# A pair's middle result taken by ScalarE before the seventh product, and its sum of weights formed by GpSimd

## The chip, the cores and the metric

The kernel runs on one core of a Trainium2 chip. The metric is the device time of one execution, in microseconds (us); shorter is better. Five engines work side by side, each through its own queue in order, and wait for one another by semaphores: TensorE (PE in the profile, its weight loads PEld), VectorE (DVE), ScalarE (ACT), GpSimd (POOL) and SyncE (SP), which here issues DMAs.

## The reference

One layer of a hybrid decoder: 16 meta tokens stand before 512 tokens of width 1024, and on the same RMS-normalised stream run a differential softmax attention and a chunked gated DeltaNet, whose gated outputs are merged. Cut to what matters:

```python
hn = rms_norm(h, norm_w)                       # 528 x 1024
proj = hn @ w_in                               # 1024 x 10256, split into:
aq, ak, av, az, dq, dk, dv, dz, db, da, ga, gd
y_a = (rms_norm(diff_attention(aq, ak, av)) * silu(az)) @ w_branch_attn
y_d = (rms_norm(gated_delta(l2(conv(dq)), l2(conv(dk)), conv(dv), ...)) * silu(dz)) @ w_branch_delta
h = h + (sigmoid(ga) * y_a + sigmoid(gd) * y_d) @ w_out
out = rms_norm(h, final_norm_w)[:, 16:]
```

Everything is float32. The change touches how blocks of `hn @ w_in` (`ak`, `av`, and most of `dk`, `dv`, `dq`) and the two branch products are computed, not what is computed.

## The kernel before, in words

**Tiles and passes.** `w_in` comes in blocks of 128 output channels, each 1024x128, held as a 128x1024 tile `raw`. To keep float32 accuracy, weights and activations are each split in a high part (`wh`, `hnH`) and a low part (`wl`, `hnL`), and a product of one 128-row slice is three matmuls: high by high, low activations by high weights, high activations by low weights (`PASSES`). ScalarE makes `wh` by a copy (a CAST of 128x1024), VectorE makes `wl` by a subtraction.

**Pairs of blocks.** Two neighbouring blocks are computed together, with seven half-size products in place of eight (Strassen's scheme in Winograd's form). The 528 tokens are cut into halves of 264 (`HALF`), the 1024 input channels into two halves. 17 pairs of `w_in` go through `pair_of_blocks`, 8 pairs of the branch weights through `pair_products`. A product is 4 slices by 3 passes, 12 matmuls of 264 columns. They run in this order, each with its accumulator in PSUM, the weights it takes, their half, and the half or sum of activations:

```python
PRODUCTS = dict(p1=("r", "wa", 0, "b11"), p2=("s", "wa", 1, "b21"), p6=("r", "wb", 1, "t2"), p5=("t", "wb", 0, "t1"),
                p7=("r", "wc", 0, "t3"), p4=("r", "wc", 1, "t4"), p3=("t", "wd", 0, "b22"))
PAIR_PRODUCTS = {**PRODUCTS, "p4": ("q", "wc", 1, "t4")}
```

So p3 is the seventh product, and it adds to the accumulator "t" that p5, the fourth, has filled. Out of the accumulators come four quarters of result: block 0 takes a copy of r after p1 plus s, and a copy of r after p6 plus t after p3; block 1 takes a copy of r after p7 (the tile `cn`, copied by ScalarE in `snap_c`) plus q, and the same `cn` plus t as it stands **before** p3. The quarters go to a tile `xp` (for blocks that a convolution follows) or `vT` (attention keys and values). `total` is the VectorE addition that makes a quarter. For the last quarter named, `total(1, 1, "t", "c", cn)`, p3 has to wait: the dense work yields `c+` until that addition has read t, and the addition itself waits for `cn`, which waits for p7.

**The sums of weights.** `split_pair` holds both raw blocks, `a1` and `a2`, and forms in VectorE additions of 128x512 the weights wb (in the tile `st`), wc (over `a2`) and wd (over half of `a1`: `raw<-raw,st` in the profile). wd is formed only after the low part of wa was made, since wa is read from the same place. Then follow its cast on ScalarE (`wh<-raw` 128x512) and its low part on VectorE (`wl<-raw,wh` 128x512). Only p3 takes wd. There are three pairs of buffers W for split weights, and wd's comes free when p2 is done.

**What sets the order.** Tasks are written as generators. A planner (`Plan`) runs them against its own table of instruction costs and hops between engines and writes each engine's instructions down in the order in which they would start; a task that waits for an event or a buffer lets others go ahead. So a change of who waits for what moves instructions of all the other tasks (DeltaNet chunks, attention heads, gates) around it. `th` is a kind of buffer of two 128x512 tiles (slices of the tile `room`), which the gates' tanh uses; its two slots are first given out when the sums of activations t1 to t4 have been formed.

Of the kernel before, what the change touches and what calls it, by code (L numbers as in the profile page):

```python
# [14 lines left out]
ALU = mybir.AluOpType  # L15
# [18 lines left out]
def dense_order():  # L34

    order = []
    for g in range(H // 2):
        k, v, q, z = ([(n, 2 * g), (n, 2 * g + 1)] for n in ("dk", "dv", "dq", "dz"))
        a0, a1 = ([(n, 2 * g + i) for n in ("ak", "av", "aq", "az")] for i in range(2))
        order += k + v + (a0 + q + a1 + z if g else q + a0[2:3] + z[:1] + a0[:2] + a0[3:] + z[1:] + a1)  # L40
    order += [("gd", c) for c in range(KB)] + [("ga", 0)]
    for n in range(KB):
        order += [("ga", n + 1)] * (n < KB - 1) + [(("yd", "ya")[n // 4], 2 * (n % 4) + i) for i in range(2)]
    return order
# [6 lines left out]
                p7=("r", "wc", 0, "t3"), p4=("r", "wc", 1, "t4"), p3=("t", "wd", 0, "b22"))  # L51
# [6 lines left out]
ORDER = dense_order()  # L58
# [3 lines left out]
HALF = L // 2  # L62
# [6 lines left out]
PE, DVE, ACT, POOL, SP = "PE", "DVE", "ACT", "POOL", "SP"  # L69
# [19 lines left out]
class Plan:  # L89
# [176 lines left out]
def hybrid_block(ctx: ExitStack, tc: tile.TileContext, x, meta, wblk, wbd, wout, pcol, prow, out):  # L266
    nc = tc.nc
    plan = Plan({**SLOTS, "wo": 0, "th": 0}, BANKS, ALL_BANKS)
    T, V, A, G, S = (Engine(plan, n, e) for n, e in
                     ((PE, nc.tensor), (DVE, nc.vector), (ACT, nc.scalar), (POOL, nc.gpsimd), (SP, nc.sync)))  # L270
    spawn, done = plan.spawn, plan.done
# [127 lines left out]
    st = mk(wp, [P, D], F32, "st")  # L399
# [29 lines left out]
    def split_pair(n, two):  # L429

        (a1, i1), (a2, i2) = two
        h0, h1, both = slice(0, D // 2), slice(D // 2, D), slice(0, D)
        name = (ORDER[n][0], ORDER[n][1] // 2) if ORDER[n][0] in ("yd", "ya") else n
        pairs[name] = tiles = {}

        def sums():
            yield ("st",)
            yield DVE
            V.tensor_tensor(out=st[:, h0], in0=a2[:, h0], in1=a2[:, h1], op=ALU.add)
            yield DVE  # L440
            V.tensor_tensor(out=st[:, h1], in0=st[:, h0], in1=a1[:, h0], op=ALU.subtract)
            done(f"wb sum {name}")
            yield DVE
            V.tensor_tensor(out=a2[:, h0], in0=a1[:, h0], in1=a2[:, h0], op=ALU.subtract)
            done(f"wc sum {name}")
            yield f"wa {name}"
            yield DVE
            V.tensor_tensor(out=a1[:, h1], in0=a1[:, h1], in1=st[:, h1], op=ALU.subtract)
            done(f"wd sum {name}")
            if tick(f"st {name}", 2):  # L450
                give("st")

        def low(key, src, cols, which):
            wh, wl = Ws[which]
            yield DVE
            V.tensor_tensor(out=wl[:, cols], in0=src, in1=wh[:, cols].bitcast(F32), op=ALU.subtract)
            tiles[key] = wh, wl, which
            done(f"{key} {name}")
            if key == "wb":
                if tick(f"st {name}", 2):  # L460
                    give("st")
            elif key != "wa":
                plan.give("raw", i2 if key == "wc" else i1)

        if n:
            yield f"took {n - 1}"
        spawn(sums())
        for key, src, cols in (("wa", a1, both), ("wb", st, both), ("wc", a2, both), ("wd", a1[:, h1], h0)):
            if key != "wa":
                yield f"{key} sum {name}"  # L470
            yield ("W",)
            which = plan.task.slot
            yield ACT
            A.copy(out=Ws[which][0][:, cols], in_=src)
            spawn(low(key, src, cols, which))
        done(f"took {n + 1}")
# [380 lines left out]
    ths = [room[3][:, n, 0:SEQ] for n in range(SLOTS["th"])]  # L857
# [11 lines left out]
    cn = mk(dp, [P, HALF], F32, "cn")  # L869
# [811 lines left out]
    WHOLE = dict(dk=whole_dk, dv=whole_dv, dq=whole_dq, ak=whole_ak, av=whole_av)  # L1681
# [196 lines left out]
    def pair_of_blocks(n):  # L1878

        (n0, i0), (n1, i1) = ORDER[n], ORDER[n + 1]  # L1880
        kind = "xp" if n0 == n1 else "vT"
        acc, to, which = {}, {}, {}
        tokens = slice(0, HALF), slice(HALF, L)

        def take(m):
            if m in which:
                yield f"to {m} {n}"
                return
            which[m] = None
            if kind == "vT":  # L1890
                yield "ap"
            yield (kind,)
            which[m] = plan.task.slot
            to[m] = xps[which[m]][:, 3:3 + L] if kind == "xp" else late["vT"][which[m]]
            done(f"to {m} {n}")

        def snap(key, m, tau):
            yield from take(m)
            yield ACT
            A.copy(out=to[m][:, tokens[tau]], in_=acc["r"])  # L1900
            done(f"{key} {n}")

        def snap_c():
            yield ("cn",)
            yield ACT
            A.copy(out=cn, in_=acc["r"])
            give("pd", acc["r"])
            done(f"c {n}")

        def total(m, tau, of, key, src=None):  # L1910

            yield f"{key} {n}"
            yield from take(m)
            yield DVE
            dst = to[m][:, tokens[tau]]
            V.tensor_tensor(out=dst, in0=acc[of], in1=dst if src is None else src, op=ALU.add)
            if of != "t" or m == 0:
                give("pd", acc[of])
            if of == "t":
                done(f"{key}+ {n}")  # L1920
            if src is not None and tick(f"cn {n}", 2):
                give("cn")
            if tick(f"block {m} {n}", 2):
                name, i = ORDER[n + m]
                spawn(WHOLE[name](i, which[m]), 1)

        follow = dict(p1=lambda: snap("a", 0, 0), p2=lambda: total(0, 0, "s", "a"), p6=lambda: snap("b", 0, 1), p7=snap_c,
                      p4=lambda: total(1, 0, "q", "c", cn), p3=lambda: total(0, 1, "t", "b"))
        for key, (bk, wt, hf, part) in PAIR_PRODUCTS.items():
            if key in ("p6", "p7"):  # L1930
                yield f"{'a' if key == 'p6' else 'b'} {n}"
            if key == "p4":
                spawn(total(1, 1, "t", "c", cn), -1)
            if key == "p3":
                yield f"c+ {n}"
            yield f"{wt} {n}"
            if part in of_sum:
                yield part
            wh, wl, which_w = pairs[n][wt]
            w = wh[:, 512 * hf:512 * hf + 512], wl[:, 512 * hf:512 * hf + 512]  # L1940
            fresh = bk not in acc
            if fresh:
                yield ("pd",)
            for k in range(KB // 2):
                if part in of_sum:
                    x_ = ts_h[of_sum[part]][:, k], ts_l[of_sum[part]][:, k]
                else:
                    x_ = [hn[j][:, k + KB // 2 * (part[1] == "2"), tokens[part[2] == "2"]] for j in range(2)]
                yield PE
                if fresh and k == 0:  # L1950
                    acc[bk] = bank("pd")[:, 0:HALF]
                for m, (a, b) in enumerate(PASSES):
                    T.matmul(acc[bk], w[a][:, k * P:(k + 1) * P], x_[b], start=fresh and k == 0 and m == 0,
                             stop=k == KB // 2 - 1 and m == 2, skip_group_check=not fresh)
            if key in LAST:
                plan.give("W", which_w)
            if key in follow:
                spawn(follow[key](), -1)
        if n == PAIRS[-1]:
            done("sums free")  # L1960
# [284 lines left out]
```

## Time and profile before

| | before |
|---|---|
| median of 3 runs | 752.92 us (752.59 to 752.99) |
| profiled execution | 751.14 us, its span 749.4 us |
| TensorE / weight loads busy | 735.4 us (98%) / 668.8 us (89%) |
| VectorE / ScalarE / GpSimd busy | 629.4 us (84%) / 516.0 us (69%) / 71.8 us (10%) |
| granted TensorE clock | 0.997 |

The profile is of one execution; its span runs from the first to the last instruction, and 1.7 us of that execution's time lie outside it. A row of the timeline gives start and duration in us, engine, operation, output<-inputs by the program's names without buffer numbers, shape, and in brackets how long the engine was idle before it and who ended that. A matmul's end is modelled and matmuls overlap, so TensorE's pace is read from the distance between starts. Almost every instruction stands under the line of a recording helper (L231), so tiles tell them apart. The 17 pairs through `pair_of_blocks` lie between about 65 and 475 us, the 8 of `pair_products` between about 560 and 700 us.

### The profile page before, as it was taken

How to read it: one execution, taken by the hardware profiler on the slowest of the kernel's cores; microseconds unless marked ns; L12 is line 12 of the kernel's file. 1: busy time of each engine (PE TensorE's matmuls, PEld its weight loads, DVE VectorE, ACT ScalarE, POOL GpSimd, SP SyncE). 2: the span in 40 equal slices, each digit the busy share in tenths (PEclk: the TensorE clock that was granted, in tenths of full speed). 3: DMA queues.
4: the chain of work that ended last, by engine and by line, in shares of the span. 5: the costliest groups of instructions: out<-in, count | busy, mean ns of one | idle time of the engine just before them, and what ended most of it. 6: DMA issues, size and time to landing. Idle time of an engine off the chain costs nothing.

```text
span 749.4 us, 14381 instructions
## 1 busy us (share of the span) xinstructions
PE 735.4 (98%) x5299; PEld 668.8 (89%) x5299; DVE 629.4 (84%) x1417; ACT 516.0 (69%) x1381; POOL 71.8 (10%) x86
## 2 busy tenths in 40 slices
PE   9999999999999999999999999999999999999996
PEld 7998988899998899998899989888988998899875
DVE  6999999899899889889989898983679879789453
ACT  6369665979974889985597997577785445546132
POOL 2202001202100301300030210000010000000001
PEclk9999999999999999999999999999999999999999
DMA  8130522215232321334032314531122343133602
GB/s 300 59 114 29 142 62 65 70 62 170 62 122 85 73 71 52 120 100 141 29 72 72 120 56 137 212 71 58 57 66 103 142 143 113 54 108 112 231 5 108
DMA packets 45432, 74.34 MB, mean 99 GB/s; under 512 B 20729, under 2 KB 25893, under 8 KB 45362
## 3 DMA queue, kind: packets, MB, share of 16 engines
q1 hardware_dynamic: 45360, 73.43, 30.8%
q8 instruction: 41, 0.67, 0.4%
q14 instruction: 29, 0.24, 0.1%
q10 hardware_dynamic: 2, 0.00, 0.0%
HBM read 67.06 MB, written 6.36 MB: 98 GB/s over the span
## 4 chain that ended last, share of the span: by engine, by line
PE 71%; ACT 12%; DVE 11%; issue 3%; DMA 2%; SPq 0%; POOL 0%; POOLq 0%; DVEq 0%; ACTq 0%
PE bank L231 68%; DVE wl L231 3%; PE psc L231 2%; ACT wh L231 2%; ACT ak L231 1%; ACT TM L231 1%; DMA raw<-in_wblk_dram 1%; DVE tmps L231 1%; DVE ts L231 1%; DMA xt<-in_x_dram 1%; DVE y L231 1%; DVE raw L231 1%; ACT MT L231 1%; DVE ast L231 1%; ACT vr L231 1%
## 5 line engine op out<-in xcount | busy, mean ns | idle before, releaser
L231 PE MATMUL bank<-hnH,wh 128*128 128x512 f32 (+4 forms) x612 | 218.1, 361 | 2.6 <-DVE vT L231 2.1
L231 PE MATMUL bank<-hnL,wh 128*128 128x512 f32 (+4 forms) x612 | 206.1, 342 | 0.0
L231 PE MATMUL bank<-hnH,wl 128*128 128x512 f32 (+4 forms) x612 | 205.8, 342 | 0.0
L231 ACT CAST wh<-raw 128x1024 fp32r<-128x1024 f32 (+1 forms) x123 | 118.0, 960 | 50.7 <-PE bank L231 45.3
L231 DVE TENSOR_TENSOR wl<-raw,wh 128x1024 fp32r<-128x1024 f32 (+1 forms) x123 | 136.8, 1113 | 16.2 <-ACT wh L231 15.8
L231 PEld LDWEIGHTS bank<-hnH,wh 128*128 128x128 f32 x612 | 114.2, 189 | 16.2 <-DVE vT L231 2.8
L231 PEld LDWEIGHTS bank<-hnH,wl 128*128 128x128 f32 x612 | 113.8, 188 | 13.9
L231 PEld LDWEIGHTS bank<-hnL,wh 128*128 128x128 f32 x612 | 114.2, 189 | 10.0
L231 PE MATMUL bank<-sumH,wh 128*128 128x264 f32 x272 | 82.4, 303 | 0.0
L231 PE MATMUL bank<-sumH,wl 128*128 128x264 f32 x272 | 77.2, 284 | 0.0
L231 PE MATMUL bank<-sumL,wh 128*128 128x264 f32 x272 | 77.1, 283 | 0.0
L231 DVE SCALAR_TENSOR_TENSOR y<-xp,pc,y 128x528 f32<-128x528 f32 (+1 forms) x72 | 54.6, 761 | 0.5 <-ACT y L231 0.3
L231 PEld LDWEIGHTS bank<-sumH,wh 128*128 128x128 f32 x272 | 51.5, 189 | 0.6 <-issue 0.2
L231 PEld LDWEIGHTS bank<-sumL,wh 128*128 128x128 f32 x272 | 51.4, 189 | 0.0
L231 PEld LDWEIGHTS bank<-sumH,wl 128*128 128x128 f32 x272 | 51.1, 188 | 0.0
L231 ACT ACTIVATE e<-psc,ast 128x144 f32<-128x144 f32 (+3 forms) x64 | 34.5, 540 | 12.5 <-DVE ast L231 11.4
L231 PE MATMUL bank<-btH,wh 128*128 128x256 f32 x128 | 36.6, 286 | 1.0 <-ACT sn L231 0.9
L231 ACT CAST wh<-st 128x1024 fp32r<-128x1024 f32 x25 | 26.2, 1047 | 15.9 <-PE bank L231 14.6
L231 PE MATMUL bank<-btH,wl 128*128 128x256 f32 x128 | 36.1, 282 | 0.0
L231 PE MATMUL bank<-btL,wh 128*128 128x256 f32 x128 | 36.1, 282 | 0.0
L231 DVE TENSOR_TENSOR wl<-st,wh 128x1024 fp32r<-128x1024 f32 x25 | 30.7, 1229 | 6.2 <-ACT wh L231 6.2
L231 PE MATMUL psc<-ak,aq 128*128 128x264 f32 (+3 forms) x160 | 29.0, 303 | 0.4 <-ACT e L231 0.4
(381 smaller groups left out, 1723.4 us busy)
## 6 DMA issues: line engine op xcount, KB each, us to landing
raw<-in_wblk_dram SPq DMA_DIRECT2D x96, 512.0 KB, 3.5
raw<-in_wout_dram SPq DMA_DIRECT2D x8, 512.0 KB, 4.9
xt<-in_x_dram SPq DMA_DIRECT2D x4, 512.0 KB, 6.6
TM<-gcd SPq DMA_DIRECT2D x8, 256.0 KB, 5.5
xr<-in_x_dram SPq DMA_DIRECT2D x8, 256.0 KB, 6.3
out_dram<-xr SPq DMA_DIRECT2D x7, 256.0 KB, 2.3
room<-scrm SPq DMA_DIRECT2D x12, 128.0 KB, 3.4
oad<-room SPq DMA_DIRECT2D x6, 256.0 KB, 2.0
```

The source lines that it names most:

```text
L231: return real(*args, **kw)
```

## The change

It has two parts. In `pair_of_blocks`, ScalarE copies the accumulator t into a `th` tile as soon as p5 is done (`snap_t`); p3 waits for that copy alone (`t`) instead of the addition (`c+`), and the addition (`both`) takes the copy and `cn`, both from SBUF, whenever they are there. In `split_pair`, which serves all 25 pairs, the sum for wd is given to GpSimd instead of VectorE.

```diff
@@ split_pair: sums()
             yield f"wa {name}"
-            yield DVE
-            V.tensor_tensor(out=a1[:, h1], in0=a1[:, h1], in1=st[:, h1], op=ALU.subtract)
+            yield POOL
+            G.tensor_tensor(out=a1[:, h1], in0=a1[:, h1], in1=st[:, h1], op=ALU.subtract)
@@ pair_of_blocks
+        def snap_t():
+            yield ("th",)
+            which["t"] = plan.task.slot
+            yield ACT
+            A.copy(out=ths[which["t"]][:, 0:HALF], in_=acc["t"])
+            done(f"t {n}")
+
+        def both():
+            yield f"t {n}"
+            yield f"c {n}"
+            yield from take(1)
+            yield DVE
+            V.tensor_tensor(out=to[1][:, tokens[1]], in0=ths[which["t"]][:, 0:HALF], in1=cn, op=ALU.add)
+            plan.give("th", which["t"])
+            if tick(f"cn {n}", 2):
+                give("cn")
+            finished(1)
...
-            if of != "t" or m == 0:
-                give("pd", acc[of])
-            if of == "t":
-                done(f"{key}+ {n}")
+            give("pd", acc[of])
...
-        follow = dict(p1=..., p2=..., p6=..., p7=snap_c,
+        follow = dict(p1=..., p2=..., p6=..., p5=snap_t, p7=snap_c,
...
             if key == "p4":
-                spawn(total(1, 1, "t", "c", cn), -1)
+                spawn(both(), -1)
             if key == "p3":
-                yield f"c+ {n}"
+                yield f"t {n}"
```

The matmuls stay the same in number and shape; VectorE has 25 instructions fewer, GpSimd 25 more (128x512), ScalarE 17 more (`room<-bank`, 128x264). Their order changes from the first pair on.

**ScalarE at the twelfth pair.** Before, the rows around the copy of r after p7 (`cn`); `wh_23<-raw_14` is a cast of the following pair's weights, `e` are attention's exponentials, `vT` a quarter of this pair:

```order
L231 CAST wh_21_119<-raw_17_115 128x512
L231 COPY vT_95_721<-bank_4_81 128x264
L231 CAST wh_23_121<-raw_14_112 128x1024
L231 ACTIVATE e_4367,l_470_4276<-psc_4379,ast_4366 128x272
L231 ACTIVATE xp_44_169<-y_4322 128x512
L231 COPY cn_167<-bank_4_81 128x264
```

And of the changed kernel, where `room_33` is the `th` buffer:

```order
L231 ACTIVATE e_4397,l_467_4188<-psc_4399,ast_4396 128x400
L231 ACTIVATE sqk_4452,sc_2480<-bank_1_78 128x128
L231 ACTIVATE e_4398,ast_4396<-psc_4399,ast_4396 128x400
L231 COPY room_33_133<-bank_4_81 128x264
L231 CAST wh_23_121<-raw_14_112 128x1024
L231 COPY cn_167<-bank_6_83 128x264
```

The copy of t stands ahead of the next pair's cast, and the copy `cn` follows that cast.

**VectorE at the same pair.** Before, the two additions with `cn`; the first of them reads the accumulator t (`bank_1`) and releases p3, and `ts` and `tmps` are the triangular solve:

```order
L231 SCALAR_TENSOR_TENSOR y_4349<-xp_45_170,pc,y_4349 128x512
L231 TENSOR_TENSOR tmps_4445<-room_31_131,ts_3217 99x72
L231 TENSOR_TENSOR wl_24_122<-raw_14_112,wh_23_121 128x1024
L231 TENSOR_TENSOR vT_94_720<-bank_1_78,cn_167 128x264
L231 TENSOR_TENSOR vT_94_720<-bank_3_80,cn_167 128x264
L231 TENSOR_TENSOR ts_3217<-ts_3217,tmps_4445 99x24x3
```

And of the changed kernel:

```order
L231 TENSOR_TENSOR qT_4407<-qT_4407,TM_3898 128x512
L231 SCALAR_TENSOR_TENSOR y_4334<-xp_44_169,pc,y_4334 128x512
L231 TENSOR_TENSOR wl_24_122<-raw_14_112,wh_23_121 128x1024
L231 TENSOR_TENSOR vT_95_721<-room_33_133,cn_167 128x264
L231 TENSOR_TENSOR vT_95_721<-bank_5_82,cn_167 128x264
L231 TENSOR_SCALAR sc_2480<-sc_2480 128x4
```

The additions still stand behind the same low part `wl_24`, but the first now reads the copy, so the accumulator is not waited for here.

**GpSimd in the middle of the program.** Before, its rows are small powers (`ms`, `sc`, `ass`, `co`), masks (`TM`, `ts`) and fills:

```order
L231 TENSOR_TENSOR co_3505<-co_3505,mhalf 128x4
L231 TENSOR_TENSOR sc_2328<-sc_2328,phalf 128x4
L231 TENSOR_TENSOR co_3512<-co_3512,mhalf 128x4
L231 TENSOR_TENSOR sc_2328<-sc_2328,phalf 128x4
L231 TENSOR_TENSOR ms_2513<-ms_2513,phalf 32x1
L231 AFFINE_SELECT TM_3779<-TM_3779 128x512 x2
L231 TENSOR_TENSOR ass_3475<-ass_3475,mhalf 128x4
```

And of the changed kernel:

```order
L231 TENSOR_TENSOR co_3672<-co_3672,mhalf 128x4
L231 TENSOR_TENSOR sc_2480<-sc_2480,phalf 128x4
L231 TENSOR_TENSOR co_3677<-co_3677,mhalf 128x4
L231 TENSOR_TENSOR raw_15_113<-raw_15_113,st_116 128x512
L231 TENSOR_TENSOR ms_2515<-ms_2515,phalf 32x1
L231 TENSOR_TENSOR sc_2480<-sc_2480,phalf 128x4
L231 AFFINE_SELECT TM_3898<-TM_3898 128x512
L231 TENSOR_TENSOR raw_17_115<-raw_17_115,st_116 128x512
L231 AFFINE_SELECT TM_3898<-TM_3898 128x512
L231 TENSOR_TENSOR raw_14_112<-raw_14_112,st_116 128x512
L231 TENSOR_TENSOR ass_4189<-ass_4189,mhalf 128x4
```

The sums stand between the powers and masks of the DeltaNet chunks, which now come behind them in the queue.

More of the change, by code (lines that the diff above doesn't have):

```diff
@@ L1908, in snap_c, with finished @@
             done(f"c {n}")
+        def snap_t():
[14 more added lines that the diff above has]
+            finished(1)
+        def finished(m):
+            if tick(f"block {m} {n}", 2):
+                name, i = ORDER[n + m]
+                spawn(WHOLE[name](i, which[m]), 1)
         def total(m, tau, of, key, src=None):
@@ L1916, in total @@
             V.tensor_tensor(out=dst, in0=acc[of], in1=dst if src is None else src, op=ALU.add)
-            if of != "t" or m == 0:
-                give("pd", acc[of])
-            if of == "t":
-                done(f"{key}+ {n}")
+            give("pd", acc[of])
             if src is not None and tick(f"cn {n}", 2):
                 give("cn")
[L1923 to L1927, printed above, removed]
+            finished(m)
+        follow = dict(p1=lambda: snap("a", 0, 0), p2=lambda: total(0, 0, "s", "a"), p6=lambda: snap("b", 0, 1), p5=snap_t, p7=snap_c,
                       p4=lambda: total(1, 0, "q", "c", cn), p3=lambda: total(0, 1, "t", "b"))
```

## The prediction

> **What bounds the kernel now.** I read the page first, for the busy times and the chain that ended last:
>
> ```profile
> span 749.4 us, 14381 instructions
> PE 735.4 (98%) x5299; PEld 668.8 (89%) x5299; DVE 629.4 (84%) x1417; ACT 516.0 (69%) x1381; POOL 71.8 (10%) x86
> ...
> PE 71%; ACT 12%; DVE 11%; issue 3%; DMA 2%; SPq 0%; POOL 0%; POOLq 0%; DVEq 0%; ACTq 0%
> ```
>
> TensorE is busy for 735.4 of 749.4 us and carries 71% of the chain. The change leaves its matmuls as they are, so only its idle time can be won: 14.0 us, much of it at the start and the end. So I next read what TensorE and its weight loads waited for, from the list of waits:
>
> ```profile
> PE bank L231 <- DVE vT L231: 2.1, 3, 0.8
> ...
> PE bank L231 <- DVE xp L231: 0.2, 1, 0.2
> ```
>
> ```profile
> PEld bank L231 <- DVE vT L231: 2.8, 3, 1.0
> ...
> PEld bank L231 <- ACT pmT L231: 1.5, 4, 0.6
> PEld bank L231 <- DVE tdmt L231: 1.3, 2, 1.2
> ...
> PEld bank L231 <- ACT TM L231: 0.8, 2, 0.4
> ```
>
> The columns are total us, times, longest. A tile `vT` or `xp` that VectorE releases is a quarter of a pair. The timeline at the longest but one of these waits, on TensorE, its weight loads, VectorE and ScalarE in turn:
>
> ```profile
> 344.15 0.28 PE L231 MATMUL bank<-sumH,wh 128*128 128x264 f32 x1
> 344.27 0.28 PE L231 MATMUL bank<-sumL,wh 128*128 128x264 f32 x1
> ...
> 345.48 0.28 PE L231 MATMUL bank<-sumH,wl 128*128 128x264 f32 x1
> 346.51 0.39 PE L231 MATMUL bank<-hnH,wh 128*128 128x264 f32 x1 [0.75 <-DVE vT L231]
> 346.74 0.28 PE L231 MATMUL bank<-hnL,wh 128*128 128x264 f32 x1
> ```
>
> ```profile
> 265.51 0.19 PEld L231 LDWEIGHTS bank<-hnH,wh 128*128 128x128 f32 x1 [0.41 <-DVE xp L231]
> ...
> 346.51 0.19 PEld L231 LDWEIGHTS bank<-hnH,wh 128*128 128x128 f32 x1 [0.96 <-DVE vT L231]
> ```
>
> ```profile
> 344.89 1.22 DVE L231 TENSOR_TENSOR wl<-raw,wh 128x1024 fp32r<-128x1024 f32 x1
> 346.02 0.77 DVE L231 TENSOR_TENSOR vT<-bank,cn 128x264 f32<-128x264 f32 x2
> ```
>
> ```profile
> 344.76 0.37 ACT L231 COPY cn<-bank 128x264 f32<-128x264 f32 x1
> ```
>
> The matmul that starts late (`hnH,wh` behind the last `sumH,wl`) is the first of p3. ScalarE had copied `cn` by 345.13, but VectorE was in a low part of another block until 346.11, so the addition that p3 waits for came late. From start to start TensorE lost 1.03 us where 0.12 is its pace, and the next step of 0.23 lost 0.11 more: 1.02 us. The idle time of the weight loads in that place, 0.96, is nearer to this than TensorE's own 0.75; I count with it. Four of 17 pairs stall so: 2.8 us in three, 0.41 in the fourth, 3.2 us in all.
>
> **Part one: p3 waits for ScalarE's copy of t.** The copy can run when p5 is done, and p7 and p4 lie between p5 and p3 in every pair: 24 matmuls at 0.12 us, at least 2.9 us. Before, two steps on two engines had to fit behind p7, into the 12 matmuls (1.4 us) of p4. The price of one step and of its queue is in the groups by form:
>
> ```profile
> L231 ACT CAST wh<-raw 128x1024 fp32r<-128x1024 f32 x98 | 102.4, 1046 | 48.5 <-PE bank L231 43.1 <-DMA raw<-in_wout_dram 2.3 <-issue 1.4
> ...
> L231 ACT COPY cn<-bank 128x264 f32<-128x264 f32 x17 | 6.4, 377 | 2.9 <-PE bank L231 2.7
> ```
>
> A copy of this shape takes 0.377 us; behind a whole cast of 1.05 us it ends 1.4 us after p5, half of its cover. So the four stalls go: **3.2 us won**. By TensorE's own idle time it is 2.1 + 0.2 = 2.3, and with all bubbles behind the restart (0.11 each) 3.6; these are the bounds. What is late next at p3 is the low part of wd, below. The cover of the copy fails only if ScalarE runs over 1.5 us late behind that cast, or both `th` slots are held; each such case would cost what it is late, no more than the 1.0 us seen now.
>
> The 17 copies cost ScalarE 17 x 0.377 = 6.4 us. It is 69% busy, but not everywhere, as the sums by stretch show (columns: TensorE, weight loads, VectorE, ScalarE, GpSimd, each with its count):
>
> ```profile
> 60.00:80.00 20.00, 19.76 (x123) 17.37 (x122) 19.40 (x31) 19.87 (x50) 3.65 (x3) 1.00 0.05 9
> 80.00:480.00 400.00, 395.38 (x3064) 366.16 (x3063) 364.97 (x878) 318.04 (x926) 49.33 (x48) 1.00 0.31 95
> 560.00:700.00 140.00, 138.99 (x925) 126.73 (x924) 119.73 (x198) 70.76 (x108) 0.00 (x0) 1.00 0.36 120
> ```
>
> From 60 to 80 it is full (19.87 of 20), so a copy there delays what is behind it by 0.38; one or two pairs are concerned. From 80 to 480 it has 20% to spare. I take 0.1 us, bounds 0 and 0.8 (two copies). The copy also stands ahead of the next pair's cast, which so comes 0.38 later; that pair's p1 is three products (36 matmuls, 4.3 us) away, which hides it.
>
> The addition of cn and t no longer releases TensorE. It reads both from SBUF where t came from PSUM; the shape is the same, and nobody but the convolution or attention head of its block waits for it.
>
> **Part two: the sum for wd on GpSimd.** VectorE loses 25 sums:
>
> ```profile
> L231 DVE TENSOR_TENSOR raw<-raw,st 128x512 f32<-128x512 f32 x25 | 17.1, 686 | 0.1
> ```
>
> That frees 17.1 us of 629. Of its path, the tightest of the 25 pairs shows the slack between the sum and the cast that reads it:
>
> ```profile
> 678.89 0.69 DVE L231 TENSOR_TENSOR raw<-raw,st 128x512 f32<-128x512 f32 x1
> ```
>
> ```profile
> 682.29 0.62 ACT L231 CAST wh<-raw 128x512 fp32r<-128x512 f32 x1
> ```
>
> The sum ends at 679.58, the cast starts at 682.29: 2.7 us. The trace has no two-input sum of 128x512 on GpSimd; the nearest rows are masks, read and written there:
>
> ```profile
> L231 POOL TENSOR_SCALAR_AFFINE_SELECT TM<-TM x8: 699/1229/1980, 67.4 to 441.9; 128x512 f32<-128x512 f32 x8
> ```
>
> I take the median, 1.23 us, bounds 0.70 and 1.98; even the last is only 1.3 us longer than 0.69, inside 2.7. So the path costs nothing, unless something ahead in GpSimd's queue waits. GpSimd is 10% busy; the masks and powers behind the sums (`sc`, `ms`, `TM`) come 1.2 us later each time one is in front, which DeltaNet's chunks would feel only where TensorE waits for them (`TM`, 0.8 us in all).
>
> The other side is that GpSimd and VectorE hinder one another. Rows of three views, the tile `ak`, VectorE and GpSimd at 377.8:
>
> ```profile
> L231 DVE TENSOR_TENSOR ak<-vT,ak x16: 690/704/1251, 94.6 to 500.2; 64x528 fp32r<-64x528 f32 x16
> ```
>
> ```profile
> 377.83 1.25 DVE L231 TENSOR_TENSOR ak<-vT,ak 64x528 fp32r<-64x528 f32 x1
> ```
>
> ```profile
> 377.81 1.92 POOL L231 TENSOR_SCALAR_AFFINE_SELECT ts<-ts 32x352 f32<-32x352 f32 x2
> ```
>
> A subtraction with both inputs in SBUF, 704 ns as a rule, took 1251 where it met a mask: 0.55 us lost. The Trainium skill has a rule for this, in SBUF — State Buffer, section Who interferes with whom: VectorE's second input in SBUF comes through a read interface shared with GpSimd, and whoever starts first keeps it for its whole instruction. The row agrees. By the skill's GPSIMD Engine Reference, section 3.1, a sum of 2048 float32 takes GpSimd 4497 ns, so that 512 would take 1.1 us (an estimate); if VectorE always lost that, it would lose 28 us for the 17.1 freed and be 11 us worse off.
>
> By the rows: 25 x 0.55 = 13.8 us lost against 17.1 freed leaves VectorE 3.3 us better; bounds are nothing lost (17.1 better) and a whole 1.23 each time (30.8 lost, 13.7 worse). VectorE has 35 us idle from 80 to 480 and nothing on p3's path any more, so I take 0 for TensorE. At best the other waits that VectorE releases go too (`tdmt`, 1.3 us).
>
> **Moved work.** The planner puts all tasks in a new order. The waits in the pairs' stretch that are not p3's (weight loads on `pmT`, `tdmt`, `TM`: 1.5 + 1.3 + 0.8 = 3.6 us) stand where no other work was at hand, and the new order may add or remove some. I take a tenth of them as lost, 0.4, with bounds of half of them either way (1.8).
>
> **The sum.** -3.2 + 0.1 + 0 + 0.4 = -2.7 us. The profiled 751.14 would become 748.4; against the median, 752.92 - 2.7 = **750.2 us**. The profiled execution is 1.8 us under the median, which I take as the spread of conditions and not of the change.
>
> **The rivals.**
>
> *The waits come back elsewhere.* TensorE reaches its next dependence 3.2 us earlier, while ScalarE and VectorE have no less to do before it; in the chain, ScalarE and VectorE together have 23%. For it speaks that 3.6 us of other waits stand among the pairs already, each on a product of ScalarE or VectorE. Against it: in the pairs' stretch both engines have idle time (35 and 82 us of 400). If three quarters of the win is lost so, 0.8 us are left: 752.1 us. The same result comes if p3 merely waits for the new copy, at 0.15 us in each of 17 pairs (2.6 us). Chance 0.25.
>
> *VectorE is blocked on the path.* If each sum blocks VectorE for 1.23 us and frees 0.69, VectorE is 0.54 later 17 times in the pairs' stretch, 9.3 us. Its place is the low parts `wl` of wa and wb, which p1 to p5 wait for. For it: VectorE is 97% busy from 60 to 80 and 91% from 80 to 480; nearly all its long work has two inputs in SBUF. Against it: at 377.8 the loss was 0.55, less than what a sum frees, and a mask also waited itself (1980 against 699). By the Trainium skill's rule above (SBUF — State Buffer, Who interferes with whom) this is what happens wherever GpSimd starts first. It decides when over a third of the 9.3 us reaches TensorE (3.2 / 9.3); with 60% it is 5.6 - 3.2 + 0.5 = 2.9 slower: 755.8 us. Chance 0.13.
>
> *The copy does not come early.* The planner could put it late on ScalarE. The order speaks against it: in the place shown it stands ahead of the cast and of `cn`. This is in the first rival's chance.
>
> **How the numbers follow.** The forecast, 750.2, has 0.62. A run of this kernel can tell about 0.2% from no change, 1.5 us: faster is under 751.4, slower over 754.4. The forecast's own range is 3.6 + 1.3 at best, 748.0, to 751.4 at worst; the first rival lies in the middle band, the second beyond it. The range for 8 in 10 takes the lower end at 747.8 (3.6 won at p3 and 1.5 of other waits) and reaches up through the first rival to 754.2, the second's milder cases. Faster 0.62, same 0.25, slower 0.13.
>
> **What would show it.** In the profile of the changed kernel: no wait of TensorE or weight loads on VectorE's `vT` or `xp` before an `hnH,wh` of 128x264, and none on `room<-bank`; 17 rows of `room<-bank` 128x264 at about 0.38 us; 25 rows of `raw<-raw,st` on GpSimd near 1.2 us; VectorE's busy time between 612 and 643. The prediction is wrong if TensorE's idle total is not 2 to 4 us under 14.0, or if `wl` rows lengthen and TensorE waits for them.

## The result, and the profile after

The changed kernel takes **758.93 us** (median of 4 runs, 757.71 to 759.11) where the kernel before, run beside it, takes 752.75 (4 runs, 751.85 to 752.99): a ratio of 1.0081, 95% interval 1.0063 to 1.0098. It is 6.1 us slower, 4.7 to 7.4, where 2.7 us faster was predicted. The profiled execution took 759.11 us. Its page, with the busy times and the chain that ended last:

```profile
span 757.4 us, 14420 instructions
PE 739.3 (98%) x5299; PEld 668.2 (88%) x5299; DVE 631.3 (83%) x1392; ACT 519.9 (69%) x1398; POOL 114.3 (15%) x111
...
PE 56%; DVE 23%; ACT 12%; issue 4%; DMA 3%; SPq 0%; POOL 0%; DVEq 0%; POOLq 0%; ACTq 0%
```

Two things are to be seen. VectorE's share of the chain has gone from 11% to 23%. And its busy time has not fallen: 25 sums of 686 ns, 17.1 us, were taken from it, and it is busy for 631.3 us where it was 629.4. So 19 us have come onto its other instructions. TensorE's idle time has gone from 14.0 to 18.1 us. That is half of the 8.0 us by which this profile is longer; the other 3.9 us stand in TensorE's busy time, with the same matmuls, whose ends are modelled.

The groups by form hold the two things that the change adds:

```profile
L231 POOL TENSOR_TENSOR raw<-raw,st 128x512 f32<-128x512 f32 x25 | 40.1, 1605 | 272.7 <-DVE wl L231 258.9 <-issue 9.8 <-DVE ms L231 2.9
...
L231 ACT COPY room<-bank 128x264 f32<-128x264 f32 x17 | 6.5, 379 | 2.9 <-PE bank L231 2.9
```

The copies are there at 379 ns. The sum on GpSimd takes 1605 ns in the mean; the tile's own view gives shortest, median and longest (the last section shows what made the longest so long):

```profile
L231 POOL TENSOR_TENSOR raw<-raw,st x25: 1275/1300/5636, 65.0 to 684.5; 128x512 f32<-128x512 f32 x25
```

And the list of what the weight loads waited for:

```profile
PEld psc L231 <- ACT e L231: 4.1, 7, 1.0
PEld bank L231 <- issue: 3.2, 12, 0.4
PEld psc L231 <- ACT ak L231: 2.5, 3, 1.1
PEld bank L231 <- DVE tdmt L231: 2.3, 3, 1.0
PEld bank L231 <- ACT sn L231: 2.1, 6, 0.7
PEld bank L231 <- ACT pmT L231: 2.0, 5, 0.6
PEld bank L231 <- ACT xp L231: 1.9, 3, 1.0
PEld bank L231 <- ACT vT L231: 1.2, 2, 0.7
```

The wait on VectorE's `vT` (2.8 us before) and the one on its `xp` are gone, as the change intends, and there is none on `room<-bank`. Other waits are new or longer: on attention's exponentials `e` (0.6 before) and keys `ak`, on `tdmt` (1.3 before), on `pmT` (1.5 before), and on ScalarE's `xp` and `vT`. In the three longest of the seven waits on `e`, 2.5 of the 4.1 us, ScalarE itself had stood idle for VectorE just before; before most of the others, and before the casts of `ak`, it came from other work without a gap. The longest wait on `xp` is at 19.68 us, ahead of the pairs. The other two and both on `vT` are inside the pairs, where the kernel before has none: p6 or p7, which adds to the accumulator r, waits until ScalarE has copied r as it stands. One of them, ScalarE's copy and the first matmul of p6:

```profile
204.78 0.36 ACT L231 COPY xp<-bank 128x264 f32<-128x264 f32 x1
```

```profile
205.19 0.39 PE L231 MATMUL bank<-sumH,wh 128*128 128x264 f32 x1 [0.37 <-ACT xp L231]
```

So in four places a pair still waits, 2.0 us by the idle time of the weight loads, for another copy than the one that the change added. The sums by stretch show where TensorE is idle:

```profile
80.00:480.00 400.00, 391.71 (x3023) 359.59 (x3023) 358.08 (x833) 320.02 (x948) 71.84 (x64) 1.00 0.29 88
560.00:700.00 140.00, 139.54 (x911) 126.40 (x910) 121.87 (x195) 75.54 (x120) 15.57 (x8) 1.00 0.33 110
```

From 80 to 480, where the 17 pairs lie, TensorE is idle for 8.3 us where it was 4.6. From 560 to 700, where the other 8 pairs lie with their 8 sums, it is idle for 0.5.

### The profile page after: what moved, and what is told of

Same layout as the page of the kernel before. It is cut to its first block, busy times and chain, and to the rows that moved or that the text cites. A ratio compares the mean times of both kernels' runs of the same rounds, so it can differ in the third digit from the quotient of the medians.

```text
span 757.4 us, 14420 instructions
## 1 busy us (share of the span) xinstructions
PE 739.3 (98%) x5299; PEld 668.2 (88%) x5299; DVE 631.3 (83%) x1392; ACT 519.9 (69%) x1398; POOL 114.3 (15%) x111
## 4 chain that ended last, share of the span: by engine, by line
PE 56%; DVE 23%; ACT 12%; issue 4%; DMA 3%; SPq 0%; POOL 0%; DVEq 0%; POOLq 0%; ACTq 0%
PE bank L231 54%; DVE wl L231 6%; DVE tmps L231 2%; DVE ts L231 2%; ACT wh L231 2%; PE psc L231 2%; DMA raw<-in_wblk_dram 2%; DVE y L231 2%; DVE ast L231 2%; ACT TM L231 1%; ACT ak L231 1%; DVE st L231 1%; DVE room L231 1%; ACT MT L231 1%; ACT vr L231 1%
## 5 line engine op out<-in xcount | busy, mean ns | idle before, releaser
L231 POOL TENSOR_TENSOR raw<-raw,st 128x512 f32<-128x512 f32 x25 | 40.1, 1605 | 272.7 <-DVE wl L231 258.9
```

Source lines behind the costliest of these rows:

```text
L231: return real(*args, **kw)
```

## The experiments

Two theories stood at the start. **A:** GpSimd's sums block VectorE, and TensorE waits for what VectorE then brings late. **B:** the planner's new order, made for both edits, brings other waits. A trace of the changed kernel alone can't tell them apart, since every engine's order differs. A ratio is always to the kernel before on the same chip, with its 95% interval; one in a thousand is 0.75 us.

### One part at a time, planned anew

The copy alone (the sum for wd back on VectorE), and the sum alone (p3 waiting for `c+` as before). Both are written as in the change, so the planner makes an order of its own for each.

```diff
 split_pair of the changed kernel, e1_copy_only
-            yield POOL
-            G.tensor_tensor(out=a1[:, h1], in0=a1[:, h1], in1=st[:, h1], op=ALU.subtract)
+            yield DVE
+            V.tensor_tensor(out=a1[:, h1], in0=a1[:, h1], in1=st[:, h1], op=ALU.subtract)
 split_pair of the kernel before, e2_sum_only
-            yield DVE
-            V.tensor_tensor(out=a1[:, h1], in0=a1[:, h1], in1=st[:, h1], op=ALU.subtract)
+            yield POOL
+            G.tensor_tensor(out=a1[:, h1], in0=a1[:, h1], in1=st[:, h1], op=ALU.subtract)
```

> The copy of t by ScalarE alone; the sum for wd stays on VectorE; the planner orders anew. Theory A (GpSimd's sums block VectorE, and VectorE's lateness is the loss): without the sums the four stalls of p3 are won, 749 to 751 us. Theory B (the planner's new order brings waits elsewhere, whoever forms the sum): 754 to 760 us, with new waits on attention's exponentials.

> The sum on GpSimd alone; p3 waits for VectorE's addition as before; the planner orders anew. A: 757 to 761 us, as slow as both parts together, or slower, since p3's stalls stay. B: anything from 750 to 760 us, by the luck of its order.

Measured: 757.18 us, ratio 1.0067 (1.0041 to 1.0092), for the copy alone; 766.3 us, 1.0187 (1.0161 to 1.0213), for the sum alone. The copy alone lies where B had it; the sum alone lies above the ranges of both. The two add up to 19 us, three times what both cost together. So they are not two prices that can be added: each kernel has an order of its own.

### The sum alone, in the order of before; and the order of after with the sum on VectorE

From here on the order is held. In the first kernel the planner still books the sum on VectorE, so it writes the order of before, but GpSimd executes it. In the second it books the sum on GpSimd, which gives the order of after, but VectorE executes it.

```diff
 split_pair, e3_sum_old_order
             yield DVE
-            V.tensor_tensor(out=a1[:, h1], in0=a1[:, h1], in1=st[:, h1], op=ALU.subtract)
+            kw = dict(out=a1[:, h1], in0=a1[:, h1], in1=st[:, h1], op=ALU.subtract)
+            plan.spend(DVE, V.time("tensor_tensor", (), kw))
+            nc.gpsimd.tensor_tensor(**kw)
 split_pair of the changed kernel, f1_new_order_dve
             yield POOL
-            G.tensor_tensor(out=a1[:, h1], in0=a1[:, h1], in1=st[:, h1], op=ALU.subtract)
+            kw = dict(out=a1[:, h1], in0=a1[:, h1], in1=st[:, h1], op=ALU.subtract)
+            plan.spend(POOL, G.time("tensor_tensor", (), kw))
+            nc.vector.tensor_tensor(**kw)
```

> The order of before, instruction for instruction on every engine, but the 25 sums run on GpSimd: the planner is told that VectorE does them. A: VectorE is blocked by more than it is freed, 755 to 760 us. B: the order is the old one, so 751 to 754 us.

> The order of the changed kernel, but the 25 sums run on VectorE where the planner thinks that GpSimd does them: no blocking, 17 us more of VectorE. A: faster than the changed kernel, 750 to 755 us. B: as slow as the changed kernel, 757 to 762 us.

Measured: 757.28 us, ratio 1.0062 (1.0041 to 1.0083), for the sum in the old order; 761.1 us, 1.0118 (1.0081 to 1.0155), for the new order with the sum on VectorE. The first is what A said and B did not: with the matmuls in the order of before, the sum on GpSimd alone costs 4.7 us. The second is not what A said. It should have been faster than the changed kernel, and it is not. The pages of the two, of the sum in the old order and of the new order with the sum on VectorE, say why:

```profile
PE 740.0 (98%) x5299; PEld 670.4 (89%) x5299; DVE 634.8 (84%) x1392; ACT 515.4 (68%) x1381; POOL 109.4 (14%) x111
```

```profile
PE 740.3 (98%) x5299; PEld 668.8 (88%) x5299; DVE 630.9 (83%) x1417; ACT 519.4 (69%) x1398; POOL 74.7 (10%) x86
```

In the order of after, VectorE is busy for 630.9 us when it forms the sums itself and for 631.3 when GpSimd does: what it is blocked for is as long as what it gave away. So the second kernel puts on VectorE what the planner had not booked there, as GpSimd's sums do, and the two times agree within their intervals. It could not tell A from B. It does show that in the order of after the sums cost no more on GpSimd than on VectorE.

### What the sum itself costs: left out, without reading, and twice

Three kernels with the matmuls, VectorE and ScalarE in the order of before. In the first the 25 sums are left out; in the second GpSimd fills the same 128x512 three times in the place of each sum, so that it is held as long but reads nothing; in the third it does each sum twice.

```diff
 e3_sum_old_order, its last line: e9_no_sum
-            nc.gpsimd.tensor_tensor(**kw)
 g1_fill_no_read
-            nc.gpsimd.tensor_tensor(**kw)
+            for _ in range(3):
+                nc.gpsimd.memset(a1[:, h1], 0.0)
 g2_sum_twice
+            nc.gpsimd.tensor_tensor(**kw)
             nc.gpsimd.tensor_tensor(**kw)
```

> The order of before without the 25 sums for wd on any engine (p3 takes weights that lack it): VectorE freed of 17.1 us, GpSimd as before. If e3 lost its 4.5 us to GpSimd's blocking, this is as fast as before or faster, 749 to 752; if a late or changed wd cost it, as slow as e3, 756 to 757.

> The order of before; in place of each sum for wd, GpSimd fills the same 128x512 three times (wd is left out of the result): about as long in GpSimd's queue as a sum, at the same place and with the same waits, but nothing is read from SBUF. If the 7 us between e9 and e3 come from GpSimd's reads blocking VectorE, this is as fast as e9, 749 to 752, and VectorE's rows keep their usual lengths. If they come from what stands behind the sums in GpSimd's queue, or from wd's later date, it is as slow as e3, 756 to 758.

> As e3, with each sum on GpSimd done twice (the second takes st away once more, so wd is not what it should be): twice the reads. By blocking, 3 to 7 us more than e3: 759 to 764. If the sums' price is a single loss of order, the same as e3, 756 to 758.

Measured: 750.24 us, ratio 0.9968 (0.9952 to 0.9985), without the sums; 749.3 us, 0.9965 (0.9953 to 0.9978), with the fills; 767.55 us, 1.0206 (1.0189 to 1.0222), with each sum twice. The pages in that order:

```profile
PE 736.5 (98%) x5299; PEld 669.7 (89%) x5299; DVE 616.9 (82%) x1392; ACT 514.9 (69%) x1381; POOL 67.7 (9%) x86
```

```profile
PE 734.7 (98%) x5299; PEld 669.1 (90%) x5299; DVE 616.6 (82%) x1392; ACT 515.3 (69%) x1381; POOL 107.3 (14%) x161
```

```profile
PE 742.3 (97%) x5299; PEld 669.8 (87%) x5299; DVE 648.8 (85%) x1392; ACT 516.1 (67%) x1381; POOL 146.6 (19%) x136
```

Three things follow. GpSimd is as busy with the fills (107.3 us) as with the sums (109.4), and VectorE is as free (616.6) as with nothing there (616.9): it isn't GpSimd's time that hurts, nor the later wd, but what the sum reads. The sum costs VectorE 634.8 - 616.9 = 17.9 us, 0.72 us each, where 0.686 was taken off it. And the time goes with it: the difference of the ratios 1.0062 and 0.9968 is 7.1 us, 40% of 17.9; done twice, it costs VectorE another 14.0 us and the kernel another 10.8, more than the 3 to 7 us expected and a larger share (77%).

One place, from VectorE's block to TensorE's wait, in the kernel with the sum in the old order, then in the one with the sum left out. The rows are of GpSimd, of VectorE (a step of the triangular solve, then the row maxima), of ScalarE's exponentials and of TensorE:

```profile
95.36 1.89 POOL L450 TENSOR_TENSOR raw<-raw,st 128x512 f32<-128x512 f32 x1 [21.86 <-DVE wl L231]
```

```profile
95.91 0.18 DVE L231 TENSOR_TENSOR tmps<-room,ts 99x29 f32<-99x29 f32 x1
96.12 0.28 DVE L231 TENSOR_TENSOR vm<-bank,vm 16x128 fp32r<-16x128 f32 x1
96.43 0.88 DVE L231 TENSOR_TENSOR ts<-ts,tmps 99x29 f32<-99x29 f32 x1
...
104.12 0.45 DVE L231 TENSOR_REDUCE ast<-psc 128x2 f32<-128x288 f32 x1
```

```profile
104.61 0.38 ACT L231 ACTIVATE e<-psc,ast 128x144 f32<-128x144 f32 x1 [1.51 <-DVE ast L231]
```

```profile
106.26 0.77 PE L231 MATMUL psc<-ak,aq 128*128 128x272 f32 x4 [1.10 <-ACT e L231]
```

```profile
94.68 0.18 DVE L231 TENSOR_TENSOR tmps<-room,ts 99x29 f32<-99x29 f32 x1
94.90 0.28 DVE L231 TENSOR_TENSOR vm<-bank,vm 16x128 fp32r<-16x128 f32 x1
95.21 0.21 DVE L231 TENSOR_TENSOR ts<-ts,tmps 99x29 f32<-99x29 f32 x1
...
102.26 0.45 DVE L231 TENSOR_REDUCE ast<-psc 128x2 f32<-128x288 f32 x1
```

```profile
104.39 0.77 PE L231 MATMUL psc<-ak,aq 128*128 128x272 f32 x4
```

The step `ts<-ts,tmps`, with both inputs in SBUF, takes 0.88 beside the sum and 0.21 without it, and ends at 97.31 with the sum's own end (97.25). From `tmps` to `ast` VectorE needs 8.21 and 7.58 us: the 0.63 are not made up on the way. From `ast` to the matmul they need 2.14 and 2.13 us, and the matmul that did not wait at all now waits 1.10. Just before it TensorE is 0.70 us behind the other kernel and just after it 1.87: VectorE was 1.23 behind at `tmps` already, and the 0.63 come on top. `vm<-bank,vm`, just ahead of the step and also beside the sum, takes 0.28 in both; it has one input in PSUM. And beside the fills the same step keeps its length (GpSimd, then VectorE):

```profile
93.01 1.70 POOL L451 MEMSET raw<- 128x512 f32 x3 [21.32 <-DVE wl L231]
```

```profile
94.11 0.22 DVE L231 TENSOR_TENSOR ts<-ts,tmps 99x29 f32<-99x29 f32 x1
```

Matmul by matmul against the kernel before, the sum in the old order is 4.5 us later at 480 us than at 21, in steps of 0.2 to 0.8 us at such waits (attention's scores, its transposes, `pmT`). From 480 us on the lag grows no more, though 8 sums of branch pairs come there and block VectorE as long: TensorE needs little of VectorE there (with each sum twice the lag grows there as well, by 1.7).

### The copy alone, in the order of before

The copy without the planner: ScalarE takes t right behind p5 (in another kernel directly ahead of the copy `cn`, behind p7) and puts it, rounded to the weights' format, in the unused half of wd's buffer; the addition reads it there. And a kernel in which the addition takes `cn` twice and t not at all, so that p3 waits for nobody and nothing is paid for it. The planner knows of neither copy: they come on top of a ScalarE order that it wrote without them.

```diff
 e4_copy_old_order
+                spare[name] = Ws[which][0][:, D // 2:D // 2 + HALF]
...
+            if key == "p5":
+                nc.scalar.copy(out=spare[n], in_=acc["t"])
...
-            V.tensor_tensor(out=dst, in0=acc[of], in1=dst if src is None else src, op=ALU.add)
+            V.tensor_tensor(out=dst, in0=spare[n].bitcast(F32) if of == "t" and m == 1 else acc[of], in1=dst if src is None else src, op=ALU.add)
 e8_no_copy
+            V.tensor_tensor(out=dst, in0=cn if of == "t" and m == 1 else acc[of], in1=dst if src is None else src, op=ALU.add)
```

> The order of before on every engine, the sums on VectorE, but ScalarE copies t behind p5 into the unused half of wd's high part (rounded there to the format of the weights, so the fourth quarter is a little less exact), and VectorE's addition reads the copy, so p3 waits for ScalarE alone. The planner knows nothing of it. If p3's four stalls are on the path and come back nowhere, 3.2 us are won: 748 to 749.5 beside 751.5 to 752.5 of before. If TensorE only waits later for it, no difference: 751 to 753. If the copies delay ScalarE, slower: 753 to 755.

> The order of before, with ScalarE's copy of t as in e4, but put directly in front of the copy of r (cn) behind p7, where ScalarE comes by anyway, so that it waits for no product in front of others. If what e4 gave away is ScalarE standing in front of a product that isn't done, this wins most of the 3.3 us at p3: 749.5 to 751 beside 752 of before. If every 0.38 us of ScalarE in front of what TensorE needs costs, wherever it stands, 753 to 755.

> The order of before, and the addition that p3 waits for takes cn twice instead of t (that quarter of the result is left out): p3 waits for nobody and nobody copies. What of the 3.3 us at p3 stays: if TensorE meets its next dependence later, 751 to 752; if the whole win stays, 749 beside 752 of before.

Measured: 755.27 us, ratio 1.0036 (1.0019 to 1.0053), with the copy behind p5; 753.55 us, 1.0018 (1.0007 to 1.0029), with the copy at `cn`; 750.57 us, 0.9985 (0.9974 to 0.9997), without a copy. So p3's waits, taken away for nothing, are worth 1.1 us (0.2 to 2.0) and not 3.2; the copy costs 3.8 us behind p5 and 2.5 us at `cn`.

Where the other 2 us of p3's waits went, the last of the four places shows. TensorE before, at p3's first matmul and at the first work behind p3, then VectorE's row that this work needs:

```profile
471.03 0.39 PE L231 MATMUL bank<-hnH,wh 128*128 128x264 f32 x1 [0.82 <-DVE vT L231]
...
472.62 0.83 PE L231 MATMUL bank<-qT,kT 128*128 128x128 f32 x6
```

```profile
471.37 0.69 DVE L231 SCALAR_TENSOR_TENSOR qT<-xp,y 128x512 f32<-128x512 f32 x1
```

And the same without the copy:

```profile
470.63 0.28 PE L231 MATMUL bank<-hnH,wh 128*128 128x264 f32 x1
...
472.68 0.71 PE L231 MATMUL bank<-qT,kT 128*128 128x128 f32 x4 [0.42 <-DVE qT L231]
```

```profile
471.94 0.69 DVE L231 SCALAR_TENSOR_TENSOR qT<-xp,y 128x512 f32<-128x512 f32 x1
```

Without p3's wait TensorE comes to `qT,kT` earlier and waits there instead, for the same VectorE: its row `qT` ends at 472.06 before and at 472.63 here, 0.57 later, just as far as this kernel was behind ahead of p3, and p3 had only been the first place to feel that queue. Matmul by matmul, the four places give 0.82, 0.47, 1.04 and 1.09 us, 3.4 in all where 3.2 was predicted, and the next dependence behind the second, third and fourth takes back 0.43 (on ScalarE's `ao`), 0.64 and 0.70.

The price of the copy has a place too. ScalarE with the copy (its cast from `bank` is the copy), and the same stretch without it:

```profile
177.53 0.19 ACT L231 ACTIVATION_READ_ACCUMULATOR sqk<-bank 128x1 f32 x1
178.03 0.38 ACT L1962 CAST wh<-bank 128x264 fp32r<-128x264 f32 x1 [0.31 <-PE bank L231]
178.30 0.40 ACT L231 ACTIVATE MT<-MT,co 128x128 f32<-128x128 f32 x1
...
193.25 0.30 ACT L231 CAST pmT<-bank 96x128 fp32r<-96x128 f32 x1
```

```profile
193.60 0.33 PE L231 MATMUL bank<-vm,pmT 96*128 96x128 f32 x1 [0.36 <-ACT pmT L231]
```

```profile
176.62 0.19 ACT L231 ACTIVATION_READ_ACCUMULATOR sqk<-bank 128x1 f32 x1
176.71 0.39 ACT L231 ACTIVATE MT<-MT,co 128x128 f32<-128x128 f32 x1
...
191.63 0.24 ACT L231 CAST pmT<-bank 96x128 fp32r<-96x128 f32 x1
```

```profile
191.93 0.33 PE L231 MATMUL bank<-vm,pmT 96*128 96x128 f32 x1
```

From `sqk` to `MT` ScalarE needs 0.77 with the copy and 0.09 without: 0.41 of waiting for p5's end and 0.27 for the copy itself (rows overlap, so a start-to-start distance is shorter than a duration). Behind it ScalarE works without a gap for 15 us, so all of it is still there at `pmT` (15.72 us from `sqk`, against 15.01), and TensorE falls 0.51 further behind there. Idle time elsewhere in ScalarE's 31% doesn't help the instruction that is next. Such a place is not the rule: behind 5 of the 17 copies ScalarE has no gap for 12 to 38 us, behind the other 12 for 1 to 7.

### Both parts in the order of before, and orders by themselves

Both edits as above, in the order of before. Then the kernel before and the changed one, each in another order of the same work: of the planner's table of hops two numbers are changed by 10 ns, and nothing else.

```diff
 b_h1, and a_h1 from the changed kernel (b_h2: DVE 120, ACT 130)
-    HOP = {PE: 200, DVE: 130, ACT: 140, POOL: 90, SP: 0}
+    HOP = {PE: 200, DVE: 140, ACT: 150, POOL: 90, SP: 0}
```

> As the kernel before it, and the sums on GpSimd too: both parts of the change in the order of before. If the two parts add, the sum's 4.5 to 5.8 us slower in the old order less what the copy wins there: 753 to 755. If GpSimd's blocking takes the copy's win as well, 757.

> The kernel before, with nothing changed but two numbers of the planner: the hops from VectorE and from ScalarE are 140 and 150 ns instead of 130 and 140. It writes another order of the same instructions. If any new order costs as much as that of the copy alone, 755 to 762 us; if orders are worth about the same, 751 to 754.

> As the kernel before it, with hops of 120 and 130 ns. The same two answers: 755 to 762 us if the old order is an uncommonly good one, 751 to 754 if not.

> The changed kernel with the planner's hops from VectorE and ScalarE at 140 and 150 ns. The same change of numbers made the kernel before 7 us slower. If the changed kernel's loss is only that it left a well chosen order, another order of it is alike: 756 to 762. If the change itself costs on top, 763 to 768.

Measured: 760.16 us, ratio 1.0108 (1.0083 to 1.0133), with both parts in the old order. The kernel before in its two other orders: 759.6 us, 1.0096 (1.0059 to 1.0132), and 759.7 us, 1.0097 (1.0068 to 1.0126). The changed kernel in another: 769.74 us, 1.0234 (1.0207 to 1.0262).

So the two parts cost 8.1 us together in the old order, more than expected but near the 4.7 + 2.7 = 7.4 that they cost one by one, and the changed kernel with its own order costs 6.1. A new order is thus not needed to explain the loss: the same work costs as much or more in the old one. But B is not excluded, since an order by itself is worth as much as either part. Another order of the unchanged work costs 7 us, and one of the changed kernel 11.5 on top of its 6.1 (two runs each); of three orders of the unchanged work, the one of before is the best. That the copy alone and the sum alone came out at 5.0 and 14.1 us, each in an order of its own, fits this. Under the same two numbers the changed kernel is 10 us slower than the one before (1.0234 and 1.0096), again with each in an order of its own.

## Why the prediction was wrong

The ledger, with the order held (differences of ratios, by 752.75 us; single terms are uncertain by 1 to 2 us, and some come from different chips):

| term | predicted | measured | from |
|---|---|---|---|
| p3's waits gone | -3.2 | -1.1 | no copy |
| ScalarE's 17 copies | +0.1 | +3.8 (at `cn`: +2.5) | copy behind p5, less no copy |
| VectorE rid of 25 sums | 0 | -2.4 | sum left out |
| GpSimd's sums hinder VectorE | 0 | +7.1 | sum in the old order, less sum left out |
| sum of these | -3.1 | +7.4 | both in the old order: +8.1 |
| moved work | +0.4 | -2.0 | changed kernel (+6.1), less both in the old order |

The traces, matmul by matmul from 21 us on, give for the same terms -1.3, +4.8 (at `cn` +1.5), -2.3, +6.9, and +8.3 for both in the old order.

**What was right.** p3's four waits were 3.2 us (3.4 matmul by matmul), and they are gone. The 17 copies take 379 ns (0.38 predicted), the typical sum on GpSimd 1.30 us (1.23), no wait on wd stands in the list, and VectorE's busy time, 631.3, lies between 612 and 643 (but 1.9 above 629.4, where 3.3 below was taken). So the edits did what they were said to do, and the time went the other way; of the prediction's own signs TensorE's idle total failed, 18.1 us where 10 to 12 were wanted.

**The step that failed** is that idle time takes up what is added: on ScalarE in part one (below, under the copies), where the term was off by 2.4 to 3.7 us, and on VectorE in part two, where it was off by 4.7. In part two it reads: "VectorE has 35 us idle from 80 to 480 and nothing on p3's path any more, so I take 0 for TensorE". Both halves of the exchange were counted as VectorE's busy time, the balance came out 3.3 us better, and idle time was taken to absorb the rest. Two things were false. The loss was 0.72 us a sum and not the 0.55 of the one row taken, since 22 of 25 sums met a VectorE instruction that grew, by up to 1.1 us (counted in the kernel with the sum in the old order); those that grew had two inputs in SBUF, down to steps of 0.2 us. Of the other three sums two met no VectorE instruction, and one met four, each with an input in PSUM, and none of them grew. And VectorE's lateness isn't absorbed by idle time that lies elsewhere: 40% of it came out at TensorE, in the place shown by way of `ast`, `e` and the scores. What was given away returned less: 17.1 us off VectorE's busy list, 2.4 us of time, 0.9 of it at p3's own waits. Why a block costs TensorE more than the same time given back isn't shown; the planner had booked the sums on VectorE and doesn't know of the blocks.

**The second rival** (VectorE is blocked on the path) was right in its mechanism and was given 0.13. Its size was wrong: it counted VectorE 0.54 us later a sum, block less relief, where the two nearly cancel (0.72 less 0.686), and it is the block that reaches TensorE (40%) more than the relief (14%). Its place was wrong too: not the low parts `wl` of wa and wb, for which no wait stands in the list, but attention and DeltaNet. The rule of the Trainium skill that stood beside it (SBUF — State Buffer, section Who interferes with whom: VectorE's second SBUF input goes through a read interface shared with GpSimd, held for a whole instruction by whoever starts first) agrees with these runs: the step beside the sum waited until the sum was over, 0.88 for 0.21; one with an input in PSUM kept its 0.28; and fills that read nothing cost VectorE nothing.

**The first rival** (the waits come back elsewhere) was right of p3: 2.1 of the 3.2 us were handed back (1.2 to 3.0), two thirds where the rival had three quarters. The prediction weighed it against the engines' idle totals, which was the same mistake.

**The copies.** "From 80 to 480 it has 20% to spare" priced 17 instructions of 0.38 at 0.1 us. In the old order they cost TensorE 0.15 to 0.22 us each. In the place shown ScalarE works without a gap from the copy to a product that TensorE takes, and 20% of idle time elsewhere can't help there. What they cost in the order of after, which the planner wrote with the copies in it, wasn't measured by itself.

**Moved work.** 0.4 with bounds of 1.8 was far too narrow: for one and the same work the orders tried differ by 7 us, one of them by 11. The planner's new order happened to be about 2 us better than the old one for this work, on intervals that overlap.

What stays open: why one order costs 7 us more than another was not looked into, so how good the order of after is for its work is only known by the few tried. How the order of after would do without GpSimd's reads (the fills in that order) and a planner that books a block on VectorE for each sum weren't tried. No kernel here with the whole computation is faster than the one before; the nearest, with the copy at `cn` and the sum on VectorE, is 0.18% slower (0.07 to 0.29).

## What to carry to other kernels

Giving an engine's instruction to GpSimd frees that engine only if what stays there doesn't share what GpSimd reads through; price the move by the rows that lie beside GpSimd's existing instructions, all of them and not one, before counting the busy time as won. Idle time in total is no slack: look for the gap between the added instruction and the next product that a bound engine takes, and where there is none, expect its duration to arrive there. And where a planner or a scheduler rewrites the order, compare in a held order (book one engine, execute on another), and run one or two neighbouring orders of the unchanged kernel to see what an order alone is worth.

## What the runs showed of the hardware

A block is not in proportion to the blocked instruction. A subtraction with both inputs in SBUF that starts behind GpSimd's sum takes most of what is left of the sum on top of its own time, whether it is long (`wl<-st,wh`, 2.32 us for 1.22, 1.10 of the 1.23 left) or short (0.88 for 0.21, 0.67 of the 0.82 left), in the kernel with the sum in the old order:

```profile
631.99 2.32 DVE L231 TENSOR_TENSOR wl<-st,wh 128x1024 fp32r<-128x1024 f32 x1
```

```profile
631.60 1.62 POOL L450 TENSOR_TENSOR raw<-raw,st 128x512 f32<-128x512 f32 x1 [12.61 <-DVE wl L231]
```

It goes the other way too: a sum that starts behind VectorE's work took 1.6 to 1.9 us in these rows where the shortest is 1.27. And it can go on for long. The longest sum of the changed kernel met eight VectorE instructions with two inputs in SBUF, each starting before the one ahead had ended; it ended 1.16 us after the last of them. The sum, then the first and the last of the eight:

```profile
570.78 5.64 POOL L231 TENSOR_TENSOR raw<-raw,st 128x512 f32<-128x512 f32 x1 [12.97 <-DVE wl L231]
```

```profile
570.62 0.69 DVE L231 TENSOR_TENSOR raw<-raw,raw 128x512 f32<-128x512 f32 x1
...
574.57 0.69 DVE L231 TENSOR_TENSOR b2L<-room,b2H 128x512 fp32r<-128x512 f32 x1
```

Part one made more VectorE work that can be blocked: the addition that read t in PSUM reads both inputs in SBUF in the changed kernel, and three of the 17, two beside a sum and one beside a mask, took 0.85 to 1.24 us where the others, and all of the kernel before, take 0.43 or a little less. Nine of them (shortest, median, longest):

```profile
L231 DVE TENSOR_TENSOR xp<-room,cn x9: 421/430/1242, 142.7 to 468.3; 128x264 f32<-128x264 f32 x9
```

Three fills of the same tile took 1.70 us together and blocked nothing.

In some profiles, among them those of the sum in the old order, the sum left out, the copy behind p5 and no copy, the first 20 us are 1.5 to 1.7 us longer, since the matmuls there stay at half pace for longer (the two of `bank<-nrow,ones` take 0.96 us from the first to the next product in the kernel before, 1.87 with the sum in the old order); lags between kernels were counted from 21 us on for that reason. What sets it wasn't looked into.
